# Query and key projections of the third head group by seven block products in the last two of four heads

## The chip, the cores and the metric

The kernel runs on one NeuronCore of a Trainium2 chip. The metric is the device time in microseconds (us) of one execution. Engines: PE is TensorE (matmuls; PEld its weight loads), DVE is VectorE, ACT is ScalarE, POOL is GpSimd, SP is SyncE, whose queue issues the loads of weights. Each engine works through its own list of instructions in a fixed order and waits for others by semaphores.

## What is computed

One layer of an encoder on a sequence of 512 tokens with 1024 features, in float32. The normalised input `n` is multiplied by one combined weight matrix; its columns give two gMLP branches (u, v), queries, keys and values of attention, and two gates. Attention has four heads in each of three groups; the groups differ in window and dilation, and their outputs are mixed per head by softmax denominators. Cut to what matters:

```python
n = rms_norm(x)
P = n @ W_in                # columns: gMLP u | gMLP v | q | k | v | gates
A = u * (W_s @ LN(v) + b_s) # gMLP gating, chunks of 128 positions
for g in range(3):          # (window, dilation) = (128,1), (512,4), (2048,16)
    q_g, k_g = rope(q[g]), rope(k[g])        # 4 heads of 128 features
    out_g, lse_g = windowed_attention(q_g, k_g, v[g])
B = mix(out_0, out_1, out_2, by softmax denominators)
h = x + rms_norm((gate_A * (A @ W_a) + gate_B * (B @ W_b)) @ W_out)
y = h + rms_norm(relu(rms_norm(h) @ W_up) ** 2 @ W_down)
```

The change concerns `q` and `k` of group 2, each of them, for a head, a 128 × 1024 by 1024 × 512 product.

## The kernel before

**Numbers.** Each float32 operand of a matmul is split into a high and a low part; a product is done as three matmuls, high by high, high by low, low by high (`mm3`, L82). `wsplit` (L69) makes the parts: ACT copies the high part (L74), DVE subtracts it from the source for the low part (L75). `split_into` (L78) does the same into given tiles (L79, L80).

**Stages.** Value projections come first (up to L294). Between them `four_sums` (L265) makes four combinations of the activations' blocks; with three blocks taken as they are they form `nmov`, the seven moving operands. Then come four heads, `project_qk(h)` and `mix(h)` (L640). After these `token_major` (L695) computes the gMLP's `v` in four accumulators `pv`, while a loop over four groups (L699) computes `u` in `pf`, does head 3's attention in pieces (`attend_steps`), and multiplies the normalised `vln` by the spatial weights into `pg` (L718). Then come the gates, the output projection and the two large feed-forward products.

**A head.** `project_qk(h)` (L437) loads q's and k's weights of a group in one tile `qkw` of 512 KB (L448). Groups 0 and 1 go through `seven_qk` (L394): the 2 × 2 block product of (q, k) by (half the features) by (half the tokens) is formed by seven block products instead of eight. `seven` (L336) prepares seven weight operands: three additions of blocks on DVE (L339, L340, L344), which need a sum tile `s` from the same buffers as the raw weights (`wsum`, L391; pool of 3), two splits of sums (L341, L345) and three of single blocks (`split1`, L386). Each `product` (L349) is 12 matmuls of 256 columns; they accumulate in three banks `pg`, and copies and joins on ACT and DVE (L409 to L426) put the results together. Group 2 in all four heads goes through `feature_tile` (L296): for q and for k 24 matmuls of 512 columns, from a split of the raw weights (L457), and two copies on ACT (L460). Then follow the rotary step (L428), the scores (L504, L516) and the softmax (L495).

**Mixing.** `mix(h)` (L531) brings both softmax sums together: small matmuls `pp` (L538) and `pc` (L561), and in between and behind some ten small DVE instructions, among them `xc` (L559), `xd` (L563) and `ca` (L565). The probabilities are scaled on ACT, `p,cf` (L567) and `p,ca` (L571). For heads 0 to 2 the latter is held back until the next head's first product has been copied; for head 3 it follows at once (L572). The transposes of head 3's probabilities (L594) need `p,ca`.

**Gating.** `evac_v` (L685) takes each `pv` through a tanh form of GELU: square (L661) and tanh (L663) on ACT, two DVE steps (L662, L664), statistics (L689, L691), a reciprocal root with one step on POOL (L96), and the normalisation (L693). `spatial_weights` (L668) transposes small tiles (`ptr`, L670; `pt` of `wsp`, L674) in banks of the tag that `pv` also uses.

**Order.** A scheduler in the framework chooses the order of each engine's instructions when the program is built, from the data, the buffers and its own estimate of times; `issue_after` in the source adds some fixed orders. So a change at one place can move instructions elsewhere. In the changed kernel every line from 451 on has a number one higher; the text uses the numbers of before.

Of the kernel before, what the change touches and what calls it, by code (L numbers as in the profile page):

```python
# [24 lines left out]
NH = 4  # L25
# [11 lines left out]
def block_kernel(ctx: ExitStack, tc: tile.TileContext, x, norm_mix_pre, w_in, b_gate, ln_v_gain, ln_v_bias,  # L37
# [25 lines left out]
    def wload(shape, srcs, name):  # L63
        raw = wpool.tile([P] + shape, F32, name=name, tag="raw")
        for dst, src in srcs(raw):
            nc.sync.dma_start(dst, src)
        return raw

    def wsplit(raw, pl=None, bufs=None, tag="w", sub=None):  # L69
        pl = pl or wpool  # L70
        shape = list(raw.shape)
        hi = pl.tile(shape, F32R, name="hi", tag=tag + "hi", bufs=bufs)
        lo = pl.tile(shape, F32R, name="lo", tag=tag + "lo", bufs=bufs)
        nc.scalar.activation(hi, raw, AF.Copy)  # L74
        (sub or nc.vector).tensor_tensor(lo, raw, hi.bitcast(F32), op=ALU.subtract)  # L75
        return hi, lo
# [219 lines left out]
    def feature_tile(wh, wl, nk, mh, ml, tag="acc"):  # L296
        ps = psA.tile([P, S], F32, name="pf", tag=tag, bufs={"acc": 4, "S": 2, "T": 1, "y": 1}[tag])
        for k in range(nk):
            mm3(ps, (wh[:, k], wl[:, k]), (mh[:, k], ml[:, k]), k == 0, k == nk - 1)
        return ps  # L300

    def fcols(wap, c0, nk, n, raw=None):
        return wap[:, c0:c0 + n].rearrange("(k p) c -> p k c", p=P)
# [6 lines left out]
    def load_v(h):  # L310
        hs = slice(h * HD, (h + 1) * HD)
        v0, v12 = vpool.tile([P, 2, 4, HD], F32R, name="v0s"), vpool.tile([P, 2, 4, HD], F32, name="v12s")
        nc.gpsimd.dma_start(v0.rearrange("p a b c -> p (a b) c"), v0d[:, :, :, hs].rearrange("p a b c -> p (a b) c"))
        for g in range(2):
            nc.gpsimd.dma_start(v12[:, g], v12d[g, :, hs].rearrange("(l r) c -> l r c", r=4))
        heads[h] = v0, v12
# [111 lines left out]
    def rotate(st, tiles, r0):  # L428
        rows = slice(r0, r0 + 32 * len(tiles))
        sw = apool.tile([P, S], F32, name="sw")  # L430
        nc.vector.stream_shuffle(sw[rows], st[rows], [(i + 16) % 32 for i in range(32)])
        nc.vector.tensor_tensor(st[rows], st[rows], rope[rows, 0], op=ALU.mult)
        nc.vector.tensor_tensor(sw[rows], sw[rows], rope[rows, 1], op=ALU.mult)
        nc.vector.tensor_tensor(st[rows], st[rows], sw[rows], op=ALU.add)
        return [nc.scalar.activation(d[0:32], st[r0 + 32 * i:r0 + 32 * i + 32], AF.Copy) for i, d in enumerate(tiles)]

    def project_qk(h):  # L437
        got, tiles, r0 = {}, [], 0
        load_v(h) if not h else None
        st = apool.tile([P, S], F32, name="st", bufs=2)  # L440
        for g in range(3):
            if g == 2:
                st, tiles, r0 = apool.tile([P, S], F32, name="st", bufs=2), [], 64
                if h:
                    attend(h - 1)
                    load_v(h)
            hd0 = (g * NH + h) * HD
            raw = wload([KD, 2, P], lambda r: [(r[:, :, 0], fcols(w_in, COL_Q + hd0, KD, P)), (r[:, :, 1], fcols(w_in, COL_K + hd0, KD, P))], "qkw")  # L448
            pair = [apool.tile([P, S], F32, name=f"{nm}{g}") for nm in "qk"]
            if g < 2:  # L450
                seven_qk(raw, g, *pair)
            for j, d in enumerate(pair):
                i = r0 + 32 * len(tiles)
                if g < 2:
                    nc.scalar.activation(st[i:i + 32], d[0:32], AF.Copy)
                else:
                    ps = feature_tile(*wsplit(raw[:, :, j]), KD, nhn, nln)  # L457
                    view = ps.rearrange("p (l r) -> p r l", r=4)
                    for dst, src in ((st[i:i + 32], view[0:32]), (d, view)):
                        nc.scalar.activation(dst.rearrange("p (r l) -> p r l", r=4), src, AF.Copy)  # L460
                tiles.append(d)
                got["qk"[j], g] = d.rearrange("p (r l) -> p r l", r=4)
            if g:
                back = rotate(st, tiles, r0)
                if g == 1 and h == NH - 2:
                    behind.extend(back[2:])
            if g == 1:
                scores_a(h, split_qk(tiles[:2]))
        scores_b(h, got)

    def split_qk(tiles):
        got = {}
        for nm, t in zip("qk", tiles):
            w = S if nm == "q" else S + P
            o = 0 if nm == "q" else ROT
            hi = apool.tile([P, w], F32R, name=f"{nm}0h")
            lo = apool.tile([P, w], F32R, name=f"{nm}0l")
            split_into(hi[:, o:o + S], lo[:, o:o + S], t)
            if nm == "k":
                for z, y in ((hi, nc.scalar), (lo, nc.vector)):  # L480
                    zf = z.bitcast(F32)
                    for dst, src in ((z[:, 0:ROT], zf[:, S:S + ROT]), (z[:, S + ROT:], zf[:, ROT:2 * ROT])):
                        if y is nc.scalar:
                            y.activation(dst, src, AF.Copy)
                        else:
                            y.tensor_copy(dst, src)
            got[nm, 0] = (hi, lo)
        return got
# [15 lines left out]
    def scores_b(h, got):  # L504
        md = small.tile([P, 2, 4], F32, name="mdb", bufs=2)
        stat[h, "md", "b"], stat[h, "m", "b"], stat[h, "d", "b"] = md, md[:, 0], md[:, 1]
        for r2 in range(2):
            ps = psA.tile([P, 2, 2, P], F32, name="psb", tag="S", bufs=2)
            for rr in range(2):
                r = 2 * r2 + rr  # L510
                for g in (1, 2):
                    nc.tensor.matmul(ps[:, rr, g - 1], got["q", g][:, r], got["k", g][:, r], start=True, stop=True)
            for rr in range(2):
                softmax_tile(h, "b", 2 * r2 + rr, ps[:, rr], masks[:, 4:6])

    def scores_a(h, got):  # L516
        md = small.tile([P, 2, 4], F32, name="mda", bufs=2)
        stat[h, "md", "a"], stat[h, "m", "a"], stat[h, "d", "a"] = md, md[:, 0], md[:, 1]
        (qh, ql), (kh, kl) = got["q", 0], got["k", 0]
        for c2 in range(2):  # L520
            ps = psA.tile([P, 2, 2, P], F32, name="psa", tag="S", bufs=2)
            for cc in range(2):
                c = 2 * c2 + cc
                qs, ks = slice(c * P, (c + 1) * P), slice(c * P, c * P + 2 * P)
                mm3(ps[:, cc], (qh[:, qs], ql[:, qs]), (kh[:, ks], kl[:, ks]), True, True)
            for cc in range(2):
                c = 2 * c2 + cc
                m = (masks[:, 0:3:2], masks[:, 1:3], masks[:, 1:3], masks[:, 1:4:2])[c]
                softmax_tile(h, "a", c, ps[:, cc], m)
# [47 lines left out]
    def attend(h):  # L577
        for _ in attend_steps(h):
            pass
# [60 lines left out]
    for h in range(NH):  # L640
        project_qk(h)
        mix(h)
# [56 lines left out]
    for g2 in range(2):  # L699
        raw = wload([KD, 2 * P], lambda r: [(r, fcols(w_in, COL_U + g2 * 2 * P, KD, 2 * P))], "uw")  # L700
        for j in range(2):
            g = 2 * g2 + j
# [376 lines left out]
    def h_split(src, first=False):  # L1079
        hl = (d0pool if first else dpool).tile([P, 2, 4, 256], F32R, name="hhl", tag="hhl")  # L1080
        with tc.issue_after(late[0].ins), tc.issue_after(late[1].ins):
            his.append(nc.scalar.activation(hl[:, 0], src, AF.Copy))  # L1082
            lows.append(nc.vector.tensor_tensor(hl[:, 1], src, hl[:, 0].bitcast(F32), op=ALU.subtract))  # L1083
        return hl[:, 0], hl[:, 1]
# [23 lines left out]
    for c in range(NC):  # L1108
        h = h_split(a11[c], c == 0)
# [169 lines left out]
```

## Time and profile before

| what | us |
|---|---|
| median of 3 runs | 779.63 |
| the three runs | 778.51, 779.63, 780.25 |
| the profiled execution | 777.72 |
| its span in the profile | 775.9 |

The profiled execution's own time lies 1.82 us above its span and 1.91 below the median of the runs. All durations in the text come from it. In a row of a timeline the first number is the start in us from the span's start, the second the duration in us; in a row of groups stand the busy time and the mean duration in ns; in a row of windows the busy time of each engine and the number of instructions. `out<-in` names the tiles, then the shape. Matmuls overlap, so a matmul's duration is longer than the distance to the next.

### The profile page before, as it was taken

What the parts mean: (1) busy time and instruction counts of PE and PEld (TensorE: products, weight loads), DVE (VectorE), ACT (ScalarE), POOL (GpSimd) and SP (SyncE); (2) the same over time, 40 slices, a digit from 0 to 9 for tenths busy, and PEclk for the clock granted to TensorE, in tenths of its full rate; (3) what the DMA queues carried; (4) which work ended last, traced back from release to release, by engine and by line L of the source; (5) the groups of instructions that cost most, each with busy time, mean ns of one, the idle gap of its engine ahead of it and who ended that gap; (6) DMA issues with size and microseconds to landing.
All of it is one profiled execution on the core that took longest, in us unless ns stands there. A gap on an engine that the chain in (4) does not pass through costs nothing.

```text
span 775.9 us, 12292 instructions
## 1 busy us (share of the span) xinstructions
PE 767.6 (99%) x4823; PEld 690.4 (89%) x4823; DVE 602.4 (78%) x963; ACT 460.5 (59%) x747; POOL 89.7 (12%) x125
## 2 busy tenths in 40 slices
PE   9999999999999999999999999999999999999996
PEld 6888999999988889999998899999999988888885
DVE  7884679888764978768756569998888699978784
ACT  6352467978776546445444457566666766655670
POOL 3310200010104400000000210011211100203010
PEclk9999999999999999999999999999999999999998
DMA  9743734262725423334444624569998998979703
GB/s 297 263 123 112 202 108 109 62 169 76 224 70 145 141 82 87 105 82 122 145 148 134 212 85 134 161 197 286 208 268 223 234 309 313 195 248 216 211 0 110
DMA packets 104749, 128.30 MB, mean 165 GB/s; under 512 B 3265, under 2 KB 75233, under 8 KB 103794
## 3 DMA queue, kind: packets, MB, share of 16 engines
q1 hardware_dynamic: 83920, 83.50, 34.1%
q0 software_dynamic: 20480, 43.61, 23.2%
q8 instruction: 38, 0.62, 0.3%
q10 hardware_dynamic: 290, 0.40, 0.2%
q14 instruction: 21, 0.17, 0.1%
HBM read 117.53 MB, written 26.74 MB: 186 GB/s over the span
## 4 chain that ended last, share of the span: by engine, by line
PE 98%; ACT 1%; issue 0%; DMA 0%; DVE 0%; POOLq 0%; POOL 0%; DVEq 0%; ACTq 0%
PE pacc L1002 13%; PE pg L353 10%; PE pd L1093 6%; PE pd L1094 6%; PE pd L1095 6%; PE pgacc L353 6%; PE pf L85 5%; PE pf L84 5%; PE pf L86 5%; PE ptp L1002 5%; PE pv L85 4%; PE pv L86 4%; PE pv L84 4%; PE pgS L353 3%; PE pd L84 2%; PE pd L86 2%
## 5 line engine op out<-in xcount | busy, mean ns | idle before, releaser
L1094 PE MATMUL pd<-hl,hhl 128*128 128x512 f32 x224 | 87.1, 389 | 0.0
L1095 PE MATMUL pd<-hl,hhl 128*128 128x512 f32 x224 | 87.0, 389 | 0.0
L1093 PE MATMUL pd<-hl,hhl 128*128 128x512 f32 x224 | 84.7, 389 | 0.0
L1002 PE MATMUL pacc<-nt,hl 128*128 128x256 f32 x504 | 66.1, 279 | 0.0
L1002 PEld LDWEIGHTS pacc<-nt,hl 128*128 128x128 f32 x504 | 61.9, 188 | 0.1
L1095 PEld LDWEIGHTS pd<-hl,hhl 128*128 128x128 f32 x224 | 42.0, 188 | 8.8
L1093 PEld LDWEIGHTS pd<-hl,hhl 128*128 128x128 f32 x224 | 42.0, 188 | 8.7
L1094 PEld LDWEIGHTS pd<-hl,hhl 128*128 128x128 f32 x224 | 42.0, 188 | 8.6
L74 ACT ACTIVATE hi<-s 128x1024 fp32r<-128x1024 f32 x30 | 31.7, 1059 | 29.6 <-DVE s L340 8.3
L75 DVE TENSOR_TENSOR lo<-s,hi 128x1024 fp32r<-128x1024 f32 x30 | 36.6, 1222 | 10.7 <-ACT hi L74 10.6
L79 ACT ACTIVATE hl<-s 128x1024 fp32r<-128x1024 f32 x28 | 29.4, 1058 | 25.7 <-DVE s L985 18.7
L80 DVE TENSOR_TENSOR hl<-dnw,hl 128x1024 fp32r<-128x1024 f32 x32 | 38.5, 1220 | 7.8 <-ACT hl L79 7.7
L84 PE MATMUL pf<-nh,hi 128*128 128x512 f32 x112 | 44.3, 396 | 0.0
L79 ACT ACTIVATE hl<-dnw 128x1024 fp32r<-128x1024 f32 x32 | 33.1, 1054 | 18.5 <-DMA dnw<-in_w_down_dram 9.9
L1002 PE MATMUL pacc<-n,hl 128*128 128x256 f32 x336 | 44.1, 279 | 0.0
L86 PE MATMUL pf<-nh,lo 128*128 128x512 f32 x112 | 44.1, 393 | 0.0
L85 PE MATMUL pf<-nl,hi 128*128 128x512 f32 x112 | 44.0, 393 | 0.0
L1002 PEld LDWEIGHTS pacc<-n,hl 128*128 128x128 f32 x336 | 41.3, 188 | 0.0
L80 DVE TENSOR_TENSOR hl<-s,hl 128x1024 fp32r<-128x1024 f32 x28 | 34.2, 1220 | 5.2 <-ACT hl L79 5.1
L85 PE MATMUL pv<-lo,nh 128*128 128x512 f32 x96 | 37.6, 391 | 0.0
L1083 DVE TENSOR_TENSOR hhl<-hid,hhl 128x1024 fp32r<-128x1024 f32 x24 | 29.3, 1220 | 10.6 <-ACT hhl L1082 10.4
L86 PE MATMUL pv<-hi,nl 128*128 128x512 f32 x96 | 37.3, 391 | 0.0
(385 smaller groups left out, 2253.5 us busy)
## 6 DMA issues: line engine op xcount, KB each, us to landing
upw<-in_w_up_dram SPq DMA_DIRECT2D x16, 1024.0 KB, 5.6
qkw<-in_w_in_dram SPq DMA_DIRECT2D x24, 512.0 KB, 5.2
dnw<-in_w_down_dram SPq DMA_DIRECT2D x12, 1024.0 KB, 6.9
gw<-in_w_in_dram SPq DMA_DIRECT2D x16, 512.0 KB, 5.4
t3d<-in_w_down_dram POOLq DMA_DIRECT2D x8, 1024.0 KB, 8.7
t1d<-in_w_down_dram POOLq DMA_DIRECT2D x8, 1024.0 KB, 9.3
slab<-in_w_in_dram SPq DMA_DIRECT2D x6, 1024.0 KB, 10.7
tsum<-in_w_down_dram POOLq DMA_DIRECT2D x6, 1024.0 KB, 9.7
```

Of the source, the lines that this page charges most:

```text
L74: nc.scalar.activation(hi, raw, AF.Copy)
L75: (sub or nc.vector).tensor_tensor(lo, raw, hi.bitcast(F32), op=ALU.subtract)
L79: nc.scalar.activation(hi, src, AF.Copy)
L80: return sub.tensor_tensor(lo, src, hi.bitcast(F32), op=ALU.subtract)
L84: nc.tensor.matmul(ps, ah, bh, start=start, stop=False)
L85: nc.tensor.matmul(ps, ah, bl, start=False, stop=False)
L86: return nc.tensor.matmul(ps, al, bh, start=False, stop=stop)
L353: nc.tensor.matmul(ps, a[:, j], b[:, j], start=first and not (j or i), stop=(j == KH - 1 and i == 2), skip_group_check=True)
L1002: ins = nc.tensor.matmul(ps, a[:, j], b[:, j], start=first and not (j or m), stop=(j == KH - 1 and m == 2), skip_group_check=True)
L1093: nc.tensor.matmul(ps, ah, bh, start=start, stop=False, skip_group_check=True)
L1094: nc.tensor.matmul(ps, ah, bl, start=False, stop=False, skip_group_check=True)
L1095: return nc.tensor.matmul(ps, al, bh, start=False, stop=stop, skip_group_check=True)
```

## The change

In heads 2 and 3 group 2's q and k go through `seven_qk` like those of groups 0 and 1:

```diff
             pair = [apool.tile([P, S], F32, name=f"{nm}{g}") for nm in "qk"]
-            if g < 2:
+            by_seven = g < 2 or h >= NH - 2
+            if by_seven:
                 seven_qk(raw, g, *pair)
             for j, d in enumerate(pair):
                 i = r0 + 32 * len(tiles)
-                if g < 2:
+                if by_seven:
                     nc.scalar.activation(st[i:i + 32], d[0:32], AF.Copy)
                 else:
                     ps = feature_tile(*wsplit(raw[:, :, j]), KD, nhn, nln)
```

With it the scheduler orders the end of head 3 and the start of the gMLP part anew. PE before, around head 3's `pc`: `pv` are matmuls of the gMLP's v, `pf` those of its first u, `pt<-ident,p` transposes of head 3's probabilities. Left out are `pv` rows like those shown.

```order
L85 MATMUL pv<-lo,nh 128x512
L561 MATMUL pc<-xc,perm 128x16
L86 MATMUL pv<-hi,nl 128x512
...
L86 MATMUL pv<-hi,nl 128x512
L84 MATMUL pf<-nh,hi 128x512
L85 MATMUL pf<-nl,hi 128x512
L594 MATMUL pt<-ident,p 128x128
L86 MATMUL pf<-nh,lo 128x512
```

PE in the changed kernel, the same place and on to the first `pg` (left out are the products of head 3's values and transposes between them):

```order
L84 MATMUL pf<-nh,hi 128x512
L562 MATMUL pc<-xc,perm 128x16
L85 MATMUL pf<-nl,hi 128x512
...
L86 MATMUL pf<-nh,lo 128x512
L595 MATMUL pt<-ident,p 128x128 x8
L671 MATMUL ptr<-ident,rows 128x32
L625 MATMUL py<-ptah,v0s 128x2x128
...
L627 MATMUL py<-ptah,v0s 128x256
L719 MATMUL pg<-wst,vln 128x128
L84 MATMUL pf<-nh,hi 128x512
```

Before, 25 matmuls of `pv` stood behind `pc`, and all 24 of the first `pf`. Now all `pv` and 19 of the 24 `pf` stand ahead of it, and the second `pf` follows only behind `pg`.

ACT before, at head 3's scaling of the probabilities (`gt<-pv` is the square, `gt<-gt` the tanh, `hi<-uw` the high part of u's weights):

```order
L571 ACTIVATE p<-p,ca 128x256 x4
L661 ACTIVATE gt<-pv 128x512 x2
L663 ACTIVATE gt<-gt 128x512
L74 ACTIVATE hi<-uw 128x1024
L663 ACTIVATE gt<-gt 128x512
```

ACT in the changed kernel at the same place:

```order
L662 ACTIVATE gt<-pv 128x512 x2
L572 ACTIVATE p<-p,ca 128x256 x4
L74 ACTIVATE hi<-uw 128x1024
L664 ACTIVATE gt<-gt 128x512 x2
L79 ACTIVATE ptah<-pt 128x512 x2
```

The two squares have moved ahead of `p,ca`; the tanh of both stays behind it.

## The prediction

> **What bounds the kernel now.** I read the page first: the busy line of the engines, the slices, the chain.
>
> ```profile
> PE 767.6 (99%) x4823; PEld 690.4 (89%) x4823; DVE 602.4 (78%) x963; ACT 460.5 (59%) x747; POOL 89.7 (12%) x125
> PE   9999999999999999999999999999999999999996
> PE 98%; ACT 1%; issue 0%; DMA 0%; DVE 0%; POOLq 0%; POOL 0%; DVEq 0%; ACTq 0%
> ```
>
> PE is full from start to end, and 98% of the chain lies on it. So time falls only if PE has fewer or shorter instructions, and any wait that the change makes on PE adds in full. Next the windows by stage: the last two attention heads are about 140 to 230 us, the mixing of head 3 and the start of the gMLP part 240 to 260.
>
> ```profile
> core 0: us, PE busy (x) PEld busy (x) DVE busy (x) ACT busy (x) POOL busy (x), PEclk, DMA share, GB/s
> 240.00:250.00 10.00, 10.00 (x51) 8.46 (x51) 4.88 (x15) 5.83 (x12) 5.37 (x6) 1.00 0.62 160
> 250.00:260.00 10.00, 10.00 (x51) 8.11 (x51) 8.16 (x18) 7.60 (x13) 6.87 (x6) 1.00 0.92 274
> 140.00:230.00 90.00, 90.00 (x644) 84.25 (x643) 71.13 (x182) 71.81 (x150) 5.91 (x8) 1.00 0.46 129
> ```
>
> PE shows no idle time in any of them; DVE has 18.9 us free of 90, ACT 18.2.
>
> **The change part by part.** *PE, removed and added.* For each of heads 2 and 3 the 48 matmuls of 512 columns (q and k, 8 blocks by 3 products each) become 84 of 256 columns (7 products of 12). Matmuls overlap, so I take the distance from start to start, not the duration. The timeline of PE, before:
>
> ```profile
> 178.17 0.40 PE L85 MATMUL pf<-nl,hi 128*128 128x512 f32 x1
> ...
> 182.51 0.39 PE L86 MATMUL pf<-nh,lo 128*128 128x512 f32 x1
> ...
> 190.01 0.28 PE L353 MATMUL pg<-nh,a 128*128 128x256 f32 x1
> ...
> 192.84 0.29 PE L353 MATMUL pg<-nh,hi 128*128 128x256 f32 x1
> ```
>
> From 178.17 to 182.51 are 19 steps of 512 columns: 0.2284 us each. From 190.01 to 192.84 are 24 steps of 256: 0.1179. One head: 48 × 0.2284 = 10.96 against 84 × 0.1179 = 9.90, so 1.06 us less, **2.1 us for both heads**. The Trainium skill ("TensorE: Matmul & The Clock Gate", section "Back-to-back issue gap") gives columns / 2.4 + 2.5 ns, which would make it 1.18 a head and 2.4 in all; the rows are slower at both sizes, and the sum keeps to them.
>
> *DVE and ACT, added.* The sums of the blocks, their low parts and the joins of the products. Groups from 100 to 245 us:
>
> ```profile
> L339 DVE TENSOR_TENSOR s<-qkw 128x1024 f32<-128x1024 f32 x5 | 6.1, 1221 | 0.1
> L340 DVE TENSOR_TENSOR s<-s,qkw 128x512 f32<-128x512 f32 x5 | 3.4, 682 | 0.0
> L344 DVE TENSOR_TENSOR s<-s,qkw 128x512 f32<-128x512 f32 x5 | 3.4, 681 | 0.0
> L80 DVE TENSOR_TENSOR ar<-qkw,ar 128x512 fp32r<-128x512 f32 x11 | 7.6, 687 | 1.1 <-ACT ar L79 1.0
> L423 DVE TENSOR_TENSOR k<-pg,u 128x256 f32<-128x256 f32 x7 | 3.0, 421 | 1.8 <-PE pg L353 1.8
> L75 DVE TENSOR_TENSOR lo<-s,hi 128x1024 fp32r<-128x1024 f32 x12 | 14.6, 1222 | 2.6 <-ACT hi L74 2.5
> L79 ACT ACTIVATE ar<-qkw 128x512 fp32r<-128x512 f32 x11 | 6.9, 627 | 1.2 <-PE pg L353 1.1
> L74 ACT ACTIVATE hi<-s 128x1024 fp32r<-128x1024 f32 x12 | 12.6, 1057 | 8.4 <-PE pf L85 4.6 <-PE pg L353 3.7
> ```
>
> The two large low parts (L75) stay, of the sums instead of the raw weights. New on DVE per head: 1.22 + 0.68 + 0.68 + 3 × 0.69 + 5 × 0.42 = 6.8 us, 13.5 for both: 18.9 us of free time shrink to 5.4. So DVE does not become the bound by its sum, but a product may stand waiting for its weights. From below that costs nothing (PE waits nowhere here now). From above: sums, high and low part in one row, 1.22 + 0.68 + 1.06 + 1.22 = 4.2 us, less the one product (12 × 0.118 = 1.4 us) that covers it, once: 2.8. ACT gets three high parts of 512 columns (0.63 each) and three copies of 256, and loses two copies of 512: under 2 us of 9.1 free per head, hidden by PE's products. The sum tile also takes one of the three raw buffers, so each head's next load starts a little later. I take **1.0 us**, nearer the lower end, since the order puts most sums at least a product ahead of their use.
>
> *The order behind the last head.* The scheduler reshuffles what follows, and this is the largest term. In both kernels the first weight matmul of the gMLP gating (`pg`, L718) waits for a chain that starts at `pc` (L561): `xd` and `ca` on DVE, four `p,ca` and then tanh on ACT, then the layer norm of `vln` on DVE. The rows of before, from the timelines of PE, ACT and DVE:
>
> ```profile
> 239.81 0.30 PE L538 MATMUL pp<-xa,perm 128*128 128x32 f32 x2
> ...
> 246.87 0.29 PE L561 MATMUL pc<-xc,perm 128*128 128x16 f32 x2
> ...
> 252.55 0.39 PE L86 MATMUL pv<-hi,nl 128*128 128x512 f32 x1
> ...
> 253.93 0.82 PE L594 MATMUL pt<-ident,p 128*128 128x128 f32 x6
> ...
> 259.23 0.24 PE L670 MATMUL ptr<-ident,rows 32*128 32x32 f32 x1
> ...
> 263.06 0.38 PE L718 MATMUL pg<-wst,vln 128*128 128x128 f32 x2
> ```
> ```profile
> 248.55 1.71 ACT L571 ACTIVATE p<-p,ca 128x256 f32<-128x256 f32 x4
> ...
> 252.98 1.06 ACT L74 ACTIVATE hi<-uw 128x1024 fp32r<-128x1024 f32 x1
> 253.94 0.62 ACT L663 ACTIVATE gt<-gt 128x512 f32<-128x512 f32 x1
> ```
> ```profile
> 245.19 0.17 DVE L559 TENSOR_TENSOR xc<-cf,perm 128x16 f32<-128x16 f32 x1
> ...
> 248.15 0.16 DVE L563 TENSOR_TENSOR xd<-pc,perm 128x16 f32<-128x16 f32 x1
> 248.35 0.17 DVE L565 TENSOR_REDUCE ca<-xd 128x4 f32<-128x16 f32 x1
> ...
> 255.28 0.65 DVE L662 SCALAR_TENSOR_TENSOR gt<-gt,pv 128x512 f32<-128x512 f32 x1
> 255.86 0.69 DVE L689 BATCH_NORM_STATS2 st<-vln 128x6 f32<-128x512 f32 x1
> 256.46 0.14 DVE L90 TENSOR_SCALAR rs_in<-mv 128x1 f32<-128x1 f32 x1
> 256.51 1.28 DVE L80 TENSOR_TENSOR ptal<-pt,ptah 128x512 fp32r<-128x512 f32 x2
> ...
> 258.96 0.54 DVE L693 TENSOR_SCALAR vln<-vln,mv,rs_out 128x512 f32<-128x512 f32 x1
> ...
> 260.81 2.18 DVE L693 TENSOR_SCALAR vln<-vln,mv,rs_out 128x512 f32<-128x512 f32 x1
> ```
>
> Before, the chain takes 246.87 to 259.5, and PE has work all the way: 25 `pv` matmuls up to 252.8, then the 24 of the first `pf` with transposes between, then the group from `ptr` to `pg` (259.23 to 263.06, 3.83 us). After the change 19 of the 24 `pf` stand *ahead* of `pc`, and no `pv` stands behind it. PE then has behind `pc` 5 `pf` (1.14), `pc` itself (0.13), 8 transposes (0.7) and the group from `ptr` on (3.83): 5.8 us.
>
> The chain by the same rows: `pc` 0.3, `xd` 0.2, `ca` 0.2, four `p,ca` 1.7, `hi<-uw` 0.96 (252.98 to 253.94), tanh 0.62: 4.0. In the new order DVE has then, up to the first normalised `vln`, ten operations of 512 (twice L664, two statistics, two `ptal`, twice L662, twice L664) at 0.6 (255.28 to 255.86, 255.86 to 256.46), five small ones at 0.1 and L693 at 0.54: 7.0. Together 11.0 to 11.2 against 5.8 of work: **PE idles about 5.3 us** ahead of `pg`. From below: if the tanh's and statistics overlap better by the 2 us that ACT and DVE wait for each other in my walk, 3.5; from above 7.5, should `vln` steps be drawn out as the last row was (2.18 us instead of 0.54). Everything behind `pg` (three more `pf`, the gates) stays bound by PE as it is, so nothing is won back. `pc` itself is not late: its input `xc` was written at 245.4, 5.6 us after the start of the matmul `pp` (L538) that it needs, and PE has 34 matmuls of 512 columns (7.8 us) between `pp` and `pc` in the new order.
>
> **Sum.** −2.1 + 1.0 + 5.3 = +4.2 us. Profiled execution 777.72 → 781.9; the median of the runs shown is 779.63, so **783.8**. By the terms' ends: −2.1 + 0 + 3.5 = +1.4 and −2.1 + 2.8 + 7.5 = +8.2, thus 781.0 to 787.8.
>
> **The rivals.** 0.2% is 1.6 us, about what a measurement here can tell from no change.
>
> *The mixing is covered after all (faster).* Place: `pc` to `pg`. The saving on PE is the surest term; if the wait behind `pc` were under 0.5 us and the heads' waits nothing, 2.1 us would show: 777.5. It decides at an idle time of 2.1: below, the kernel is not slower. For it: DVE and ACT were half idle from 240 to 250, so `pc`'s inputs could come so early that other work fits. Against: the chain's own steps are twice PE's work, in an order that is fixed. 0.14.
>
> *Gain and wait cancel (same).* Idle time of 1 to 3 us with little lost in the heads, by a chain of 7 to 9 us instead of 11: 779 to 781. 0.16.
>
> *The clock falls in the gap.* The end of the run shows what a pause does:
>
> ```profile
> 768.93 0.39 PE L1095 MATMUL pd<-hl,hhl 128*128 128x512 f32 x1
> ...
> 771.00:771.50 0.50, 0.00 (x0) 0.00 (x0) 0.50 (x1) 0.00 (x0) 0.00 (x0) 0.92 0.48 176
> 771.50:772.00 0.50, 0.00 (x0) 0.00 (x0) 0.50 (x2) 0.00 (x0) 0.00 (x0) 0.50 0.00 0
> ```
>
> PE ends at 769.3; about 2.1 us later its granted clock is half. My 5.3 us are in pieces (some 0.9 before the transposes, 2.0 ahead of `ptr`, 2.4 before `pg`), so the longest is just of that size. If it falls, the 12 `pf` behind `pg` (12 × 0.228 = 2.7 us) would take up to twice that: +1 to +2.7 more, about 785.7. The Trainium skill ("TensorE: Matmul & The Clock Gate", section "What's actually happening") says that a free-running window of about 3.4 us of idling halves the clock and as much of work restores it; by that rule the price would be 1.7 and the pieces too short; the row agrees that a pause of some microseconds does it. 0.14.
>
> *DVE becomes the bound in heads 2 and 3.* 5.4 us free in 90 is little: if three or four products wait 1 to 2.8 us each, the heads lose 5 rather than 1, about 787.5. Against: 18.9 us of free time are there now and the large low parts do not grow. 0.08.
>
> That the change does not take hold can be excluded: the order has 168 more matmuls of 256 columns and 96 fewer of 512.
>
> **How the numbers follow.** The main case 0.48, with the clock 0.14 and DVE 0.08: slower 0.70; same 0.16, faster 0.14. The range leaves out most of the fast case and the far end of the DVE case: 778.3 to 787.8.
>
> **What would show it.** Right: waits of PE in 250 to 266 us of 4 to 7 us, named for `vln`, `ptah` or `p,ca`; `pf` rows ahead of `pc`; DVE near 85 us busy over the two heads; PE's busy time about 2 us less. Wrong: PE full at 250 to 266 and the span shorter by 2 (the first rival), waits of `pg` (L353) for `lo` or joins over 3 us in 140 to 230 (the last), or a granted clock under 1 near 260.

## The result, and the profile after

The changed kernel takes 782.99 us (median of 7 runs, 782.41 to 785.49) against 779.63 (7 runs, 778.51 to 780.3): ratio 1.0054, interval 1.0045 to 1.0064, so 3.5 to 5.0 us slower. The medians themselves lie 3.4 us apart; the ratio is worked out from all executions and stands for 4.2. Forecast were 783.8 and +4.2. All medians and ratios here and below are of executions at the usual clock; a single one, of the kernel with the second `pf` ahead, took 842.0 us at a mean granted clock of 0.85 and is left out.

The page of the changed kernel, its busy line and the chain:

```profile
PE 769.8 (99%) x4895; PEld 695.5 (89%) x4895; DVE 608.8 (78%) x985; ACT 463.1 (59%) x755; POOL 89.9 (12%) x125
PE 93%; DVE 2%; DMA 1%; ACT 1%; issue 1%; POOL 0%; POOLq 0%; DVEq 0%; SPq 0%; ACTq 0%
```

PE has 72 instructions more (168 of 256 columns in, 96 of 512 out) and they should take 2.1 us less, yet its busy time grew by 2.2. The busy share still reads 99%. Only the chain shows a change, 98% to 93%. What PE waited for in the changed kernel (us in total, times, longest; the waits `idle` and `pv`, 1.0 and 0.2 us, which the kernel before has too, are left out):

```profile
PE ptr L671 <- DVE vln L665: 1.5, 1, 1.5
...
PE pt L192 <- DMA ident<-in_ident_c_dram: 0.9, 1, 0.9
PE pg L353 <- DVE q L426: 0.6, 1, 0.6
PE pt L608 <- DVE ptal L80: 0.3, 1, 0.3
PE pg L353 <- ACT z L417: 0.2, 1, 0.2
```

The 0.9 for `ident`, which the profiled execution of before does not have, lies in the start, ahead of anything that the change touches; of the 5.3 us between the two spans (775.9, 781.2) 4.4 are left. At the place that the forecast named, PE in the changed kernel:

```profile
249.74 0.30 PE L539 MATMUL pp<-xa,perm 128*128 128x32 f32 x2
...
257.72 0.29 PE L562 MATMUL pc<-xc,perm 128*128 128x16 f32 x2
...
259.10 1.77 PE L595 MATMUL pt<-ident,p 128*128 128x128 f32 x8
262.41 0.24 PE L671 MATMUL ptr<-ident,rows 32*128 32x32 f32 x1 [1.53 <-DVE vln L665]
...
268.68 0.46 PE L719 MATMUL pg<-wst,vln 128*128 128x128 f32 x2
```

From `pc` to `pg` are 10.96 us, with the 5.8 us of PE work that the forecast counted: 5.2 us are lost, where the list of waits names 1.8. The rest is hidden in three ways: a matmul counts as busy to its end, though the next one could have started long before; many gaps are too short to be listed as a wait; and matmuls at a lower clock count as busy for longer, and the clock fell here. The windows of 1 us in the changed kernel, PEclk third from the end:

```profile
core 0: us, PE busy (x) PEld busy (x) DVE busy (x) ACT busy (x) POOL busy (x), PEclk, DMA share, GB/s
261.00:262.00 1.00, 0.00 (x0) 0.00 (x0) 0.34 (x1) 1.00 (x3) 1.00 (x2) 1.00 0.39 90
262.00:263.00 1.00, 0.56 (x2) 0.32 (x2) 1.00 (x3) 1.00 (x3) 0.98 (x2) 0.98 1.09 328
263.00:264.00 1.00, 1.00 (x5) 0.71 (x4) 1.00 (x3) 1.00 (x3) 1.00 (x1) 0.50 1.10 338
264.00:265.00 1.00, 0.73 (x4) 0.64 (x4) 1.00 (x3) 0.68 (x2) 0.54 (x1) 0.50 1.15 338
265.00:266.00 1.00, 1.00 (x7) 1.00 (x6) 1.00 (x3) 0.49 (x1) 0.00 (x0) 0.50 1.24 397
266.00:267.00 1.00, 1.00 (x6) 0.76 (x6) 1.00 (x6) 0.97 (x3) 0.10 (x1) 0.81 0.86 295
```

The granted clock is half from 262.96 to 266.38, 3.4 us (0.04 + 3 + 0.38, each worked out from a window's mean). It cost nothing here, since DVE set the pace. DVE in the changed kernel, first and last rows of the chain:

```profile
252.61 0.17 DVE L560 TENSOR_TENSOR xc<-cf,perm 128x16 f32<-128x16 f32 x1
258.04 0.17 DVE L564 TENSOR_TENSOR xd<-pc,perm 128x16 f32<-128x16 f32 x1 [5.26 <-PE pc L562]
...
261.67 1.28 DVE L665 SCALAR_TENSOR_TENSOR vln<-gt,pv 128x512 f32<-128x512 f32 x2 [2.05 <-ACT gt L664]
...
267.99 0.54 DVE L694 TENSOR_SCALAR vln<-vln,mv,rs_out 128x512 f32<-128x512 f32 x1
```

`xc` lay ready at 252.8 and PE came to `pc` at 257.7, so DVE waited 5.3 us for PE; then PE waited for the chain, which took 257.72 to 268.53, 10.8 us. From 261.67 on DVE's rows stand without a gap. Each engine waited for the other once; that is what a fixed order does when it is some microseconds off.

### The profile page after: what moved, and what is told of

It reads as the page before. It is cut to its first block, busy times and chain, and to the rows that moved or that the text cites. A ratio compares the mean times of both kernels' runs of the same rounds, so it can differ in the third digit from the quotient of the medians.

```text
span 781.2 us, 12469 instructions
## 1 busy us (share of the span) xinstructions
PE 769.8 (99%) x4895; PEld 695.5 (89%) x4895; DVE 608.8 (78%) x985; ACT 463.1 (59%) x755; POOL 89.9 (12%) x125
## 4 chain that ended last, share of the span: by engine, by line
PE 93%; DVE 2%; DMA 1%; ACT 1%; issue 1%; POOL 0%; POOLq 0%; DVEq 0%; SPq 0%; ACTq 0%
PE pacc L1003 13%; PE pg L353 11%; PE pd L1095 6%; PE pd L1094 6%; PE pd L1096 6%; PE pgacc L353 6%; PE ptp L1003 5%; PE pf L85 4%; PE pf L84 4%; PE pf L86 4%; PE pv L85 4%; PE pv L86 4%; PE pv L84 4%; PE pgS L353 3%; PE pd L86 2%; PE pd L85 2%
## 5 line engine op out<-in xcount | busy, mean ns | idle before, releaser
L74 ACT ACTIVATE hi<-s 128x1024 fp32r<-128x1024 f32 x34 | 35.9, 1059 | 28.2 <-DVE s L340 14.7
L75 DVE TENSOR_TENSOR lo<-s,hi 128x1024 fp32r<-128x1024 f32 x34 | 41.5, 1224 | 10.8 <-ACT hi L74 10.7
L353 PE MATMUL pg<-nt,hi 128*128 128x256 f32 x240 | 44.3, 282 | 0.6 <-DVE q L426 0.6
L353 PEld LDWEIGHTS pg<-nt,hi 128*128 128x128 f32 x240 | 37.0, 188 | 1.1 <-DVE q L426 0.8
L84 PE MATMUL pv<-hi,nh 128*128 128x512 f32 x96 | 37.3, 396 | 0.0
## 6 DMA issues: line engine op xcount, KB each, us to landing
slab<-in_w_in_dram SPq DMA_DIRECT2D x6, 1024.0 KB, 11.2
```

Of the source, the lines that this page charges most:

```text
L84: nc.tensor.matmul(ps, ah, bh, start=start, stop=False)
L353: nc.tensor.matmul(ps, a[:, j], b[:, j], start=first and not (j or i), stop=(j == KH - 1 and i == 2), skip_group_check=True)
```

## The experiments

**Theory A**: the change saves 2.1 us on PE, loses about 1.4 in heads 2 and 3, and loses 5.2 between `pc` and `pg`, because the new order has the filler ahead of `pc`. **Rival B**: the new DVE work is what costs; it ends late in any order, and the gap is only where that shows. Each ratio is against the kernel before, measured alongside.

### The order mended in the changed kernel, and spoiled in the kernel before

The first run holds the first `pf` behind `pc`; nothing else is touched.

```diff
-        nc.tensor.matmul(pc, perm[:, P:2 * P], xc, start=True, stop=True)
+        mixed[h] = nc.tensor.matmul(pc, perm[:, P:2 * P], xc, start=True, stop=True)
...
-                ins = mm3(ps, (wh[:, k], wl[:, k]), (nhn[:, k], nln[:, k]), k == 0, k == KD - 1)
+                with nullcontext() if g else tc.issue_after(mixed[NH - 1].ins):
+                    ins = mm3(ps, (wh[:, k], wl[:, k]), (nhn[:, k], nln[:, k]), k == 0, k == KD - 1)
```

> The changed kernel with the 24 matmuls of the first pf held behind head 3's pc; the same instructions on every engine. Theory A (the loss is the idle time of about 5.2 us between pc and pg, because the filler was used up ahead of pc): pc comes 4.3 us earlier (19 pf of 0.228 us), the idle time falls to about 1 us, the time to 778.7 (778.2 to 779.5). Rival B (the loss is the 13.5 us of new DVE work in heads 2 and 3, which ends late whatever the order; the gap is only where it shows): within 1 us of the changed kernel, 782 to 784.

Measured: 781.5, ratio 1.0031 (1.0018 to 1.0044). Between the two: theory A's direction, a third of its size. PE in this run:

```profile
249.16 0.30 PE L540 MATMUL pp<-xa,perm 128*128 128x32 f32 x2
...
252.84 0.29 PE L563 MATMUL pc<-xc,perm 128*128 128x16 f32 x2
...
260.64 0.38 PE L626 MATMUL py<-ptah,v0s 128*128 128x256 f32 x1 [0.32 <-ACT ptah L79]
262.10 2.04 PE L679 MATMUL prs<-wst,onesq 128*128 128x512 f32 x2 [1.08 <-ACT wst L677]
...
266.89 0.39 PE L721 MATMUL pg<-wst,vln 128*128 128x128 f32 x2
```

From `pp` on, `pc` came 4.3 us earlier, as expected (3.7 us behind `pp` instead of 8.0), but `pg` only 1.2 (17.7 instead of 18.9). From `pc` to `pg` are 14.05 us for 24 × 0.228 + 4.7 = 10.1 of work. There is a wait of another kind, `prs` for `wst`, and the clock falls again; its windows in this run:

```profile
260.00:262.00 2.00, 0.70 (x4) 0.27 (x2) 2.00 (x6) 2.00 (x6) 1.98 (x3) 1.00 0.31 71
262.00:263.50 1.50, 1.40 (x2) 0.69 (x3) 1.50 (x5) 0.90 (x3) 1.50 (x1) 0.56 1.12 319
263.50:265.50 2.00, 2.00 (x9) 1.57 (x8) 1.62 (x6) 0.77 (x2) 1.27 (x3) 0.50 1.14 333
265.50:267.00 1.50, 1.50 (x14) 1.50 (x14) 1.50 (x4) 1.12 (x3) 0.00 (x0) 0.97 0.59 190
```

Half clock for 1.3 + 2.0 + 0.1 = 3.4 us, and this time PE had work in it: `prs` takes 2.04 where it took 1.02 before. That is up to 1.7 us. So theory A had left out the clock: its fall costs more after a smaller gap, when PE has work again, than after a larger one, in which PE was waiting anyway.

The other way round: the kernel before with `pc` tied behind 18 of the first `pf`.

```diff
+                if g == 0 and k == 5:
+                    tc.add_manual_dep(mixed[NH - 1].ins, ins.ins.name, ..., reason="issue_after")
```

> The kernel before, with pc of head 3 held back until 18 matmuls of the first pf are done, so that PE's order behind pc is that of the changed kernel; no other work is changed. Theory A: an idle time of about 5 us between pc and pg appears here too, 784.6 (783.8 to 785.5). Rival B: without the new DVE work ACT and DVE catch up, under 1 us of loss, 779.6 to 780.6.

Measured: 784.25, ratio 1.0069 (1.0048 to 1.0089). Without any of the new DVE work the order alone costs 3.7 to 6.9 us, as much as the whole change or more. Rival B falls for this part. PE in this run, the first normalised `vln` on DVE, and two windows:

```profile
257.07 0.29 PE L562 MATMUL pc<-xc,perm 128*128 128x16 f32 x2
...
269.53 0.50 PE L721 MATMUL pg<-wst,vln 128*128 128x128 f32 x2
```
```profile
267.34 0.53 DVE L694 TENSOR_SCALAR vln<-vln,mv,rs_out 128x512 f32<-128x512 f32 x1
```
```profile
262.00:263.00 1.00, 0.97 (x6) 0.60 (x5) 1.00 (x4) 1.00 (x3) 0.91 (x1) 0.97 0.02 8
...
269.00:270.00 1.00, 1.00 (x7) 1.00 (x7) 1.00 (x2) 0.30 (x1) 0.00 (x0) 0.62 0.07 16
```

The chain is as long as in the changed kernel, 257.07 to 267.87 or 10.8 us, so the new DVE work doesn't lengthen it. But `pg` comes only 12.5 us behind `pc`, and it no longer waits for the chain: PE's rows follow each other up to it. The clock is half in every window between the two shown, from 262.94 to 269.76, 6.8 us, and PE is late by it. So of the 6.4 us lost here (12.46 − 6.03 of work, with one `pf` more than in the changed kernel) about 4.8 are the wait for the chain and up to 1.7 the clock.

### One head at a time

```diff
-            by_seven = g < 2 or h >= NH - 2
+            by_seven = g < 2 or h == NH - 2
```

> Seven products in head 2's third group only. 25 matmuls (1 pv, 24 pf) stay behind head 3's pc. Theory A: -1.1 on PE, half of the heads' waits (+0.5 to +1) and under 1 us of idle time ahead of pg: 780.0 (779.0 to 780.7). Rival B: half of the whole loss of 3.4, so 781.3.

Measured: 781.68, ratio 1.0035 (1.0022 to 1.0048): what rival B expected, 781.3. The waits of PE in this run say where it is:

```profile
PE pg L719 <- DVE vln L694: 1.1, 1, 1.1
...
PE prs L678 <- ACT wst L676: 0.6, 1, 0.6
PE pg L353 <- DVE q L426: 0.6, 1, 0.6
PE pg L353 <- ACT z L417: 0.5, 1, 0.5
...
PE py L625 <- DVE mv L692: 0.4, 1, 0.4
```

1.1 us by name lie in head 2, 2.1 behind `pc` (253.37; `pg` at 266.83; from start to start 13.46 − 10.37 of work, 3.1). One `pv` and 24 `pf` behind `pc` were not enough; I had counted them as enough. The chain has no fixed length: in this order ACT has a high part and two squares ahead of `p,ca`, DVE one more step of 512 columns and the four that make `sbias` ahead of the first normalised `vln`, which is ready only 13.3 us behind `pc`. That two thirds of the named waits lie behind `pc` doesn't by itself decide between A and B; the next runs do.

```diff
-            by_seven = g < 2 or h >= NH - 2
+            by_seven = g < 2 or h == NH - 1
```

> Seven products in head 3's third group only. 20 pv and 24 pf stay behind pc, as many as before within five. Theory A: -1.1 on PE, no idle time ahead of pg, +0.3 to +1 in the head: 779.2 (778.5 to 779.7). Rival B: half of the loss or more, since the new DVE work lies right ahead of the mixing: 781.3 to 782.

Measured: 778.44, ratio 0.9997 (0.9987 to 1.0006). This has half of the new DVE work directly ahead of the mixing, where rival B would be worst, and no loss shows: its order keeps 20 `pv` and 24 `pf` behind `pc`, and `pg` follows at 263.19, with one wait of 0.5 us behind it (for the second `pg`). The gain of 1.1 us is not measured either; the interval reaches from 1.0 us faster to 0.5 slower.

### Filler for the gap

The second `pf` is written ahead of the spatial weights and the first `pg` (with `pf` behind `pc` as above). The rest of the loop's body becomes a function; `turn_rows` is the part of `spatial_weights` with `ptr`; the rest is written behind the second `pf`, and `prs` is tied behind that one's first half (`behind_pf`).

```diff
+    def gate(g, u):
+        pg = psA.tile([P, 4, P], F32, name="pg", tag="acc", bufs=4)
+        ...
             if g == 0:
                 with tc.issue_after(ins.ins):
-                    spatial_weights()
-            pg = psA.tile([P, 4, P], F32, name="pg", tag="acc", bufs=4)
-            ...
+                    turn_rows()
+                held = u
+                continue
+            if g == 1:
+                spatial_weights(behind_pf)
+                gate(0, held)
+            gate(g, u)
```

> As the run with pf held behind pc, and the second pf (24 matmuls, 5.5 us) is written ahead of the spatial weights and of the first pg, so that PE has it to do while it waited. All the work of the changed kernel. Theory A (the loss beside the heads' 1.4 us is waiting ahead of pg and the halved clock that follows it): no wait and no clock under 1 there, so -2.1 + 1.4 on the kernel before (778.9): 778.2 (777.5 to 778.8). Rival B (the new DVE work makes itself felt wherever PE waits next): 780.5 to 782.

Measured: 778.24, ratio 0.9992 (0.9983 to 1.0002), theory A's number; all of the new DVE work is in it. Its windows at the place that cost 5.2 us:

```profile
140.00:232.00 92.00, 91.10 (x723) 88.28 (x723) 78.88 (x198) 72.77 (x157) 5.93 (x8) 1.00 0.44 127
...
260.00:262.00 2.00, 2.00 (x9) 1.63 (x10) 2.00 (x7) 2.00 (x5) 1.98 (x3) 1.00 0.31 73
262.00:264.00 2.00, 2.00 (x10) 1.68 (x9) 1.97 (x6) 0.92 (x3) 2.00 (x2) 1.00 1.15 322
```

No idle time and a full clock there; heads 2 and 3 (first row) have the 0.9 us of idle time that they have in the changed kernel too. Whether it beats the kernel before was measured once more:

> The kernel with the second pf ahead once more, in five rounds, to see whether it beats the kernel before by more than the measurement is uncertain. By the terms -2.1 + 1.4 = -0.7 us; so a ratio of 0.9991, and an interval of 0.06% either side would just leave 1 outside.

Measured: 778.66 against 778.71, ratio 0.9996 (0.9986 to 1.0005). So the whole loss is won back, and no gain is shown.

### The clock by itself

This is the run with `pf` behind `pc`, with 14 matmuls added that nobody reads, before the wait for `wst`. They go into the bank of `ptr`; their 256 columns take in the 32 of `ptr` itself, so that part is not unused, but DVE has copied it by 260.65, before the first of them at 260.76.

```diff
+        with tc.issue_after(turned.ins):
+            for i in range(14):
+                warmer = nc.tensor.matmul(ptr[:, A], nh[:, 0, nat][:, :P], nl[:, 0, nat][:, A], start=True, stop=True, skip_group_check=True)
```

> As the run with pf held behind pc, and 14 extra matmuls of 256 columns into an unused part of the bank of ptr, between the transposes of the spatial weights and the wait for wst: they do nothing but keep PE busy. Theory A (in that run the clock halved from 262 to 265.5 us and this cost about 1.7 us, as PE had work then): the clock stays at 1 and the time falls from 781.5 to about 779.8 although work was added. Rival (the clock costs nothing, only the waits do): 781.5 or a little above.

Measured: 780.3, ratio 1.002 (1.0011 to 1.0029). The intervals of the two ratios overlap, so the times alone make it likely rather than certain; the trace is plain. PE and a window:

```profile
253.53 0.29 PE L563 MATMUL pc<-xc,perm 128*128 128x16 f32 x2
...
260.76 1.92 PE L679 MATMUL ptr<-nl,nh 128*128 128x256 f32 x14
262.83 1.10 PE L682 MATMUL prs<-wst,onesq 128*128 128x512 f32 x2
266.03 0.49 PE L724 MATMUL pg<-wst,vln 128*128 128x128 f32 x2
```
```profile
262.00:264.00 2.00, 1.97 (x12) 1.26 (x11) 2.00 (x7) 1.40 (x4) 2.00 (x2) 1.00 1.02 307
```

With 1.65 us of useless work more, `pc` to `pg` takes 12.50 us instead of 14.05; the clock stays at 1 and `prs` at 1.10. The whole spans of the two profiled executions differ by only 0.2 us (779.5, 779.7): this one, the longest of its ten, comes to `pc` 0.7 later and takes 0.7 more behind `pg`. So the gain is shown at this place; in the whole time, where the medians lie 1.2 us apart, it is likely.

### Three misses

*Low parts on POOL.* As the run with the second `pf` ahead, but the third group's three low parts of single blocks are made on POOL (in heads 2 and 3).

```diff
+        w = seven(..., split1 if g < 2 else lambda src, tag: split1(src, tag, sub=nc.gpsimd))
```

> As the run with the second pf ahead; and the three low parts of single blocks of the third group in heads 2 and 3 (6 x 0.69 us) are made on POOL instead of DVE. Theory A (the heads' 1.4 us are joins on DVE that come late because DVE is full): about 0.7 us less than the run without it, 777.5. Rival (POOL's parts, 2.4 us for 1024 columns before, come late themselves or slow DVE): the same or up to 1 us more.

Measured: 780.08, ratio 1.0016 (1.0006 to 1.0025), 1.8 us more than without it. Five of the six low parts take about 1.3 us on POOL, one 2.3; the raw weights' buffer is read for longer, and what is late next is a load:

```profile
165.48 1.27 POOL L80 TENSOR_TENSOR ar<-qkw,ar 128x512 fp32r<-128x512 f32 x1 [6.07 <-ACT ar L79]
...
169.88 2.31 POOL L80 TENSOR_TENSOR a<-qkw,a 128x512 fp32r<-128x512 f32 x1 [1.45 <-ACT a L79]
```
```profile
185.70 1.22 DVE L339 TENSOR_TENSOR s<-qkw 128x1024 f32<-128x1024 f32 x1 [2.15 <-DMA qkw<-in_w_in_dram]
```

Without POOL this wait of DVE for the load is 1.4 us, with it 2.1. Behind the sum stands the join `u` (L421), and PE now waits 0.7 us for it. That the load is late because of the buffer was not tested by itself.

*Head 3 alone with the second `pf` ahead.* The two edits above together.

> Seven products in head 3's third group only, with the second pf ahead of pg. Theory A: -1.1 on PE and next to no waits left (that run had 0.9 us of them behind pg): 777.9 (777.5 to 778.4). Rival: no better than head 3 alone, 778.4.

Measured: 780.54, ratio 1.0025 (1.0015 to 1.0034). The order had enough filler already, and the edit moved the transposes of the spatial weights behind the second `pf`; now `prs` waits for them:

```profile
270.92 1.12 PE L682 MATMUL prs<-wst,onesq 128*128 128x512 f32 x2 [1.50 <-ACT wst L679]
```

*A bank of its own for the third group.* As the run with the second `pf` ahead, but the accumulator of products 6, 7 and 4 of the third group (`Y`) takes the bank of tag T, in both heads that use seven products there.

```diff
-        Y, Z, X = [psA.tile([P, 512], F32, name="pg", tag="acc", bufs=4)[:, A] for _ in range(3)]
+        Y, Z, X = [psA.tile(..., tag=tag, bufs=nb)[:, A] for tag, nb in ((("T", 1) if g == 2 else ("acc", 4)), ("acc", 4), ("acc", 4))]
```

> As the kernel with the second pf ahead, and product 6 of the third group takes the bank of tag T instead of one of the four that the second group's products still hold. Theory A (the 0.69 us wait at 191 in head 2 is for a bank that the join L426 frees, which stands on DVE behind a low part of 1.2 us): that wait falls to 0.3 us, where the low part itself is ready; 0.3 to 0.4 us less, 777.9. Rival (weights and bank are late together): no change, 778.2.

Measured: 799.54, ratio 1.0268 (1.0254 to 1.0282). In heads 0 to 2 the transposes and `pp`, `pc` use this one bank too, and so does the first `pf`. The longest waits of PE in this run:

```profile
PE pc L563 <- DVE xc L561: 4.4, 1, 4.4
PE py L626 <- ACT ptah L79: 1.8, 2, 1.3
PE pt L596 <- ACT p L573: 1.6, 2, 0.9
```

It tells nothing of the 0.7 us that it was to remove.

## Why the prediction was right, point by point

- **PE's saving, −2.1.** Supported, not shown alone. The instruction counts are as forecast. (The formula quoted beside this term gives 1.19 us a head, not 1.18; the sum didn't use it.) With the second `pf` ahead (all the work, no gap) the ratios, 0.9992 and 0.9996, stand for 0.6 and 0.3 us under the kernel before; with the heads' 1.4 us taken off, 1.7 to 2.0 of saving are in it. The intervals, some 0.8 us either side, don't show it by themselves.
- **The heads, +1.0 (0 to 2.8).** The size held, the reason only in part. From start to start, three places in heads 2 and 3 lose 0.31 (behind the matmul at 178.2), 0.71 (190.9) and 0.36 us (216.4), 1.4 in all. I expected products to wait for weights. The waits are named for a join that had to free a bank (`q` L426) and a copy (`z` L417). DVE in the changed kernel at the largest of them:

```profile
190.14 1.22 DVE L75 TENSOR_TENSOR lo<-s,hi 128x1024 fp32r<-128x1024 f32 x1
191.27 0.42 DVE L426 SCALAR_TENSOR_TENSOR q<-pg,p 128x256 f32<-128x256 f32 x1
```

  The join stands behind the low part of a sum, and weights and bank come late together. DVE is late there, but not by its sum: its busy time rose by 6.4 us, not 13.5. I had added durations, while a DVE row starts before its predecessor has ended (from start to start the new rows are about 11.6 us), and the two long rows of before (`z` 2.35, `vln` 2.18) are short after the change (0.16, 0.54). Both stood beside a low part on POOL that began up to 0.5 us before them (242.07 for 2.38, 260.31 for 2.39). The last 1.4 us of the difference are not accounted for.
- **Behind the last head, +5.3 (3.5 to 7.5).** Held: 5.2. The order alone, put into the kernel before, costs 3.7 to 6.9 us, up to 1.7 of them by the clock; filler takes it away again. The chain agrees in both of its parts: up to the tanh 4.0 forecast and 3.95 measured (257.72 to 261.67), DVE from there 7.0 and 6.9, together 11.0 to 11.2 and 10.8. `xc` was ready early as forecast, by 4.9 us instead of 2.2.
- **The sum, +4.2.** −2.1 + 1.4 + 5.2 = +4.5, against 3.5 to 5.0 measured and 4.4 between the spans without the start.
- **The signs** that I had named fared worse than the sum. The order was as said. The waits by name are 1.8 us, not 4 to 7; DVE is busy 78.6 us from 140 to 230, not 85; PE's busy time is 2.2 us up, not 2 down; and a granted clock under 1 near 260, which was to show me wrong, came (0.50 from 262.96). By these signs alone the gap could have been missed, or put down to the clock; the distance from `pc` to `pg` shows it.
- **The rival with the clock** came true besides, and I had its effect wrong: I put it behind `pg`, at 1 to 2.7 us. It falls ahead of `pg`, while PE waits for DVE, and is back at 1 by 266.4, before `pg` at 268.7: no cost. That was luck for the forecast, which had no term for it in the main case: with `pf` behind `pc`, and with `pc` late in the kernel before, such a fall costs up to 1.7 us. The Trainium skill ("TensorE: Matmul & The Clock Gate", section "What's actually happening") has a free-running window of about 3.4 us; the times at half clock, 3.4, 3.4 and 6.8 us, agree with one and with two of them. I had argued with it that the pieces were too short for a fall; the traces speak against that argument, and so did the row in the prediction, where the clock is half 2.1 us after PE's end.
- **The rivals of a covered gap and of gain and wait cancelling** are out for the changed kernel. Of DVE as bound in the heads there is 1.4 us of the 5.

What stays open: whether the scheduler put the filler early because of its estimate for the added DVE instructions, or for another number in its model, wasn't tried; and why head 2 alone leaves so little filler was read, not tested.

## What to carry to other kernels

Where a scheduler sets the order, cost a change not only by its own instructions but by what the new order puts between an engine and the chain that it will wait for: compare the work behind the chain's start with the chain's length, here 5.8 against 11 us; the chain's length is that of one order, in another it was 13.3. To test such a reading, spoil the order in the kernel before and mend it in the kernel after; the two runs together separate the order from the work. And do not trust the busy share or the list of waits for the size of a gap: measure from start to start between two instructions that both kernels have.

## What the runs showed of the hardware that I had not expected

- The matmul clock falls after gaps much shorter than a stage: in the changed kernel after 1.5 us without a matmul (260.9 to 262.4) and little before and after it, with `pf` behind `pc` after pieces of 0.3 and 1.1 us. The length of a piece doesn't decide it: with pieces of 0.4, 0.6 and 1.1 us (head 2 alone) the clock stayed at 1, and so it did after 1.5 us with head 3 alone and the second `pf` ahead (269.4 to 270.9). Ahead of the three falls the last matmul of `pf` had ended 3.5 to 4.1 us before, with little but transposes, one product of 256 columns and waits since; in the two runs without a fall such a stretch was 3.0 and 1.9 us. But at the end of the kernel before the clock fell about 2.1 us after the last matmul, so this isn't the whole rule, and nothing here tests it. In the changed kernel, with `pf` behind `pc`, and with `pc` late in the kernel before it stayed at half for 3.4, 3.4 and 6.8 us, though PE was busy in most of that.
- Useless matmuls in a gap kept the clock at 1 and shortened the way from `pc` to `pg` from 14.05 to 12.50 us, though they are 1.65 us of work.
- The same low part of 512 columns takes 0.69 us on DVE; on POOL five took 1.27 to 1.30 and one 2.31, beside a sum on DVE (169.81 for 1.23).
